# Five RMS norms of an encoder trunk: the root reaches all partitions through DRAM instead of by products

## The chip, the cores and the metric

The kernel runs on one core of a Trainium2 chip. The metric is device time of one execution in microseconds (us), the median of several runs. PE is TensorE, DVE is VectorE, ACT is ScalarE, POOL is GpSimd, SP is SyncE, which here only issues DMAs.

## The reference

One encoder layer is applied to a prompt of 1024 tokens and a sample of 256, with 256 memory tokens each, all of width 1024 and in fp32. Every sub-layer starts with the same norm:

```python
def rmsnorm(x, w):
    xf = x.astype(jnp.float32)
    y = xf * lax.rsqrt(jnp.mean(xf * xf, -1, keepdims=True) + EPS)
    return (y * w.astype(jnp.float32)).astype(x.dtype)
...
    h = rmsnorm(x, norm_mix_w)
    proj = h @ w_in
...
    x = x + merged @ w_out
    x = x + memory_cross_attention(rmsnorm(x, norm_xa_w), rmsnorm(mem, norm_mem_w), xa_w_q, xa_w_kv, xa_w_o)
    h = rmsnorm(x, norm_ffn_w)
    gu = h @ ffn_w_gate_up
    x = x + (jax.nn.silu(gu[..., :D_FF]) * gu[..., D_FF:]) @ ffn_w_down
```

The merged value comes from a gated DeltaNet branch (with beta and decay inputs per token and head) and a spatial gating branch (gMLP). A last `rmsnorm` follows the layer and gives the output.

## The kernel before

**Layout.** Activations lie transposed: the 1024 features are 8 tiles (index k) of 128 partitions, tokens lie along the free axis. Tokens form three blocks: blocks 0 and 1 are 512 prompt tokens each, block 2 is the sample's 256. A norm over features is therefore a sum over partitions and over the 8 tiles.

**Products.** Every fp32 operand is split into a high part (rounded on ACT, line 125) and a low part (the difference, on DVE or POOL, line 126), and each product is three matmuls (line 108, which all PE work shows as its line). The names hi, lo, whi and wlo are such halves. A 128x512 slice of weights or activations that DVE or POOL splits late holds up PE at its matmuls.

**Order.** PE's order is the order in which the program emits it. A clock in the program (`K.clock`, in units of about a nanosecond of PE time) decides when a side job may emit its next piece: a job is a generator, and `yield 2800` means that it goes on when PE has been given 2800 more. The orders of DVE, ACT, POOL and SP are made by the framework's scheduler, and each engine then executes its own order strictly. A DMA that SP issues and that has to wait holds up what stands behind it on SP.

**The norm.** `Norm.add` sums squares into the tile nacc. `Norm.rest` (lines 262 to 295) then waits `lag`, sums over partitions by products with a column of ones (line 275) into a PSUM bank, and computes the root on DVE in four columns (lines 231 to 235: 1 + 9 small steps) into the tile nst, 128x4: token 128c+p lies in partition p, column c. After `lag2` it brings the root to all partitions along the free axis: four products of a broadcast column with the identity (lines 279 to 281) into a bank pb of 128x512. Then come the rows, one for each k: normally a DVE operation x * weight * pb (line 294). In the two final norms some of the rows are "shared": ACT multiplies by the weight (line 289) and POOL by the root (line 290). POOL needs the root in SBUF, so ACT copies pb into nacc first (line 286). Each row goes to a sink: a split into hi and lo, a write to DRAM (memory norm), or the output.

**The five norms.** The memory norm runs early, beside the projections of the two gates and the gMLP branch (tiles gt, ug, vg) and the computation of beta and decay (tile wk, lines 543 to 562, whose last result gm PE uses as an operand). The feed-forward norms of blocks 0 and 1 run behind the attention's output projection, whose results DVE adds to x at line 1483; x2 is then stored to DRAM by SP (line 1513). The final norms of blocks 1 and 0 run in the last 90 us, behind the second feed-forward product; there DVE adds that product's banks to x at line 2246 and splits weights and activations (tiles wlo, gs) that PE uses soon after. Their shared rows are 1, 3, 5, 7 for block 1 and 1, 4, 6 for block 0. Three norms keep their products in both kernels: the first norms of blocks 0 and 1, and the feed-forward norm of block 2.

Of the kernel before, what the change touches and what calls it, by code (L numbers as in the profile page):

```python
# [167 lines left out]
def trunk_kernel(ctx: ExitStack, tc: tile.TileContext, a):  # L168
# [68 lines left out]
    class Norm:  # L237
# [21 lines left out]
                (eng or V).tensor_tensor(out=self.acc, in0=self.acc, in1=sq, op=ALU.add)  # L259
            self.k += 1  # L260

        def rest(self, xk, wcol, sink, pace=1300, shared=(), lag=1500, ks=range(KT), inplace=False, ready=None, halves=1, lag2=2800, rooms=()):

            p, n = self.p, self.n
            nb = n // P
            yield lag
            pc = bank()
            parts = [self.acc[:, i * n : (i + 1) * n] for i in range(halves)]
            if self.apart is not None:
                parts.append(self.apart)  # L270
            for c in range(nb):
                for t in parts:
                    mm(pc[:, c : c + 1], t[:, c * P : (c + 1) * P], one, t is parts[0], t is parts[-1])
            y = p.tile([P, 4 if p is xp else 16], F32, tag="nst", name="nst", bufs=2)[:, :nb]
            ms, sc = pc[:, 4 : 4 + nb], pc[:, 8 : 8 + nb]
            V.tensor_scalar(out=ms, in0=pc[:, :nb], scalar1=1.0 / D, scalar2=EPS, op0=ALU.mult, op1=ALU.add)
            rsqrt(y, ms, sc)
            yield lag2
            pb = bank()
            for c in range(nb):  # L280
                mm(pb[:, c * P : (c + 1) * P], y[:, c : c + 1].to_broadcast([P, P]), ident)
            while ready is not None and not ready():
                yield 300
            if shared:
                rb = self.acc
                S.activation(rb, pb[:, :n], AF.Copy)
            for k in ks:
                if k in shared:
                    S.activation(xk(k), xk(k), AF.Copy, scale=sm[:, wcol + k : wcol + k + 1])
                    G.tensor_tensor(out=xk(k), in0=xk(k), in1=rb, op=ALU.mult)  # L290
                    sink(k, xk(k))
                    continue
                t = bank() if k in rooms else xk(k) if shared or inplace else p.tile([P, 512], F32, tag="nsq", name="nt", bufs=self.sq)[:, :n]
                V.scalar_tensor_tensor(out=t, in0=xk(k), scalar=sm[:, wcol + k : wcol + k + 1], in1=pb[:, :n], op0=ALU.mult, op1=ALU.mult)  # L294
                sink(k, t)
                yield pace * n / 512
# [12 lines left out]
        rsqrt(y, ms, sc)  # L309
        yield lag2  # L310

    def norm(p, xk, n, wcol, sink, pace=1300, step=700, lag=1500):
        nm = Norm(p, n)
        for k in range(KT):
            nm.add(xk(k))
            yield step
        yield from nm.rest(xk, wcol, sink, pace, lag=lag)

    def to_h(h, b, mine=(1, 3, 5, 7)):
        return lambda k, t: split(h[b][0][:, k, :], h[b][1][:, k, :], t, V if k in mine else G)  # L320
# [139 lines left out]
    def other_norms():  # L460
# [7 lines left out]
        done.add(1)  # L468
        mem = x_load(a["memT"], 0, 512, "mem")
        yield 6000  # L470
        yield from norm(xp, lambda k: mem[:, k, :], 512, S_MEM, lambda k, t: SY.dma_start(md[k], t))

    norms = K.side(other_norms())

# [975 lines left out]
    class OutProj:  # L1450
# [21 lines left out]
        def run(self, xsrc, scale, wcol, xpool, store, sinks=None, then=None, after=None):  # L1472
# [24 lines left out]
            for b, (t0, n) in enumerate(BLOCKS):  # L1497
# [17 lines left out]
                if sinks is None:  # L1515
                    norm_b = nms[b].rest(xk, wcol, to_h(hs, b), 600)
                else:
                    norm_b = nms[b].rest(xk, wcol, sinks(b, hs), PACES[b], ks=range(KT) if b != 1 else SECOND_KS, inplace=True, lag2=LAGS2[b])
                K.pending[id(hs), b] = K.side(norm_b)
            self.x = x  # L1520

# [759 lines left out]
    def last_norm(nm, b):  # L2281
# [3 lines left out]
            (SY if k % 2 else S).dma_start(a["yT"][:, k, t0 : t0 + n], t)  # L2285

        if b < 2:
            K.side(nm.rest(lambda k: x2[b][:, k, :], S_FIN, sink, PACEF, SHARED[b], LAGF[b], lag2=LAGF2[b]))
            return
        pb = bank()  # L2290
        ms, y = pb[:, :n], pb[:, n : 2 * n]
# [118 lines left out]
MIX = 6500  # L2410
A1, A2, A3, A4 = 1200, 800, 2000, 600
DEC, CONV = 1200, 600
FIRST_W, PACES, LAGS2 = 9000, (600, 1300, 600), (2800, 9500, 9500)
LAGX = (26000, 17000, 9000)
FIRST_V = (1, 3, 5, 6, 7)
LAG0, LAGF, LAGF2, PACEF = 9700, (8000, 6000, 1500), (9000, 9000, 2800), 1000
# [81 lines left out]
```

## Time and profile before

| what | value |
|---|---|
| median of 3 runs | 2188.0 us (2187.18 to 2189.63) |
| profiled execution | 2189.87 us |
| its span | 2188.1 us |
| granted PE clock, mean | 0.998 |
| root done, memory norm | 95.07 us |
| root products of the five norms, start | 95.25, 1300.24, 1341.87, 2099.51, 2133.48 us |

The span runs from the first to the last recorded instruction; the profiled execution took 1.8 us more than it. Times in the tables of the trace are us from the start of the span. In the fences below, a row of the timeline is: start, duration, engine, line, operation, output<-inputs, and how many instructions were put together; in square brackets how long the engine had been idle and what released it.

### The profile page before, as it was taken

The numbers are of one execution on the slowest core, as the hardware profiler recorded it, in microseconds if no ns is written. First come the engines' busy times: TensorE is split into PE (matmuls) and PEld (weight loads), VectorE is DVE, ScalarE is ACT, GpSimd is POOL, SyncE is SP. The second block draws the span as 40 slices with busy tenths as digits, with TensorE's granted clock in tenths as the row PEclk, the third lists the DMA queues.
The fourth block names the chain that finished last, engine by engine and source line by source line (L and its number), as shares of the span: only waits on it lengthen the run. The fifth ranks groups of instructions, "written<-read, shape, count | busy, mean of one in ns | idle before, by whom it ended". The sixth has DMA issues, their size and how long they took to land.

```text
span 2188.1 us, 31978 instructions
## 1 busy us (share of the span) xinstructions
PE 2170.4 (99%) x12184; PEld 1888.5 (86%) x12184; DVE 1357.0 (62%) x2615; ACT 885.8 (40%) x1651; POOL 592.7 (27%) x399
## 2 busy tenths in 40 slices
PE   9999999999999999999999999999999999999998
PEld 8988888888988888888988888888888888888888
DVE  7867688786874845687644546644434444378575
ACT  6533363544535553124544533332322323343454
POOL 2010100101001010042412432566666665200031
PEclk9999999999999999999999999999999999999999
DMA  5221423323244546741522421222222222493531
GB/s 194 92 93 58 112 64 91 83 65 95 73 124 119 175 127 203 246 148 41 191 68 102 168 96 64 104 83 87 82 77 80 83 98 90 143 347 122 206 112 58
DMA packets 196600, 255.14 MB, mean 117 GB/s; under 512 B 77188, under 2 KB 111572, under 8 KB 196446
## 3 DMA queue, kind: packets, MB, share of 16 engines
q1 hardware_dynamic: 179038, 228.19, 32.0%
q10 hardware_dynamic: 17408, 24.91, 3.1%
q8 instruction: 95, 1.56, 0.3%
q14 instruction: 59, 0.48, 0.1%
HBM read 179.07 MB, written 73.99 MB: 116 GB/s over the span
## 4 chain that ended last, share of the span: by engine, by line
PE 92%; DVE 4%; DMA 3%; ACT 1%; issue 1%; SPq 0%; POOL 0%; DVEq 0%; ACTq 0%; POOLq 0%
PE bank L108 91%; PE bank L121 1%; DMA t<-sgd 1%; DMA braw<-gq 1%; DMA raw<-in_w_sv 0%; DVE gb L820 0%; DMA tbd<-stage 0%; DVE U L949 0%; DVE nt L294 0%; ACT junk L518 0%; DVE aT L815 0%; DMA gb<-grd 0%; DVE lo L126 0%; DMA stage<-gtd 0%; DVE bank L294 0%
## 5 line engine op out<-in xcount | busy, mean ns | idle before, releaser
L108 PE MATMUL bank<-hi,whi 128*128 128x512 f32 (+1 forms) x1976 | 700.4, 354 | 0.2 <-DVE vg L494 0.2
L108 PE MATMUL bank<-lo,whi 128*128 128x512 f32 (+1 forms) x1976 | 686.9, 348 | 0.0
L108 PE MATMUL bank<-hi,wlo 128*128 128x512 f32 (+1 forms) x1976 | 686.6, 347 | 0.0
L108 PEld LDWEIGHTS bank<-hi,wlo 128*128 128x128 f32 x1976 | 373.6, 189 | 48.0
L108 PEld LDWEIGHTS bank<-hi,whi 128*128 128x128 f32 x1976 | 374.4, 189 | 45.8 <-issue 1.4
L108 PEld LDWEIGHTS bank<-lo,whi 128*128 128x128 f32 x1976 | 374.5, 190 | 43.0
L126 POOL TENSOR_TENSOR wlo<-raw,whi 128x1024 fp32r<-128x1024 f32 x65 | 158.0, 2432 | 293.3 <-ACT whi L125 289.2
L125 ACT ACTIVATE whi<-raw 128x1024 fp32r<-128x1024 f32 (+1 forms) x136 | 137.0, 1009 | 241.6 <-PE bank L108 216.3
L126 DVE TENSOR_TENSOR wlo<-raw,whi 128x1024 fp32r<-128x1024 f32 (+1 forms) x71 | 82.5, 1164 | 73.2 <-ACT whi L125 65.9
L108 PE MATMUL bank<-bhl,whi 128*128 128x512 f32 x408 | 126.0, 390 | 0.1
L126 POOL TENSOR_TENSOR wlo<-x,whi 128x1024 fp32r<-128x1024 f32 x40 | 96.6, 2414 | 47.5 <-ACT whi L125 47.5
L2128 DVE TENSOR_TENSOR x<-x,bank 128x512 f32<-128x512 f32 x21 | 14.5, 689 | 124.7 <-ACT x L1923 124.7
L108 PEld LDWEIGHTS bank<-bhl,whi 128*128 128x128 f32 x408 | 76.4, 188 | 16.5 <-ACT whi L125 0.5
L698 DVE SCALAR_TENSOR_TENSOR acc<-craw,sm,acc 128x510 f32<-128x510 f32 (+1 forms) x96 | 73.4, 765 | 24.6 <-ACT acc L696 22.8
L1936 DVE SCALAR_TENSOR_TENSOR t<-t,x 128x512 f32<-128x512 f32 x42 | 63.9, 1520 | 28.7 <-ACT t L1935 28.7
L108 PE MATMUL bank<-bhl,wlo 128*128 128x512 f32 x204 | 79.7, 391 | 0.8 <-DVE wlo L126 0.8
L125 ACT ACTIVATE whi<-x 128x1024 fp32r<-128x1024 f32 (+1 forms) x48 | 49.2, 1024 | 77.5 <-PE bank L108 69.6
L1945 DVE SCALAR_TENSOR_TENSOR t<-bank,t 128x512 f32<-128x512 f32 (+1 forms) x44 | 24.5, 558 | 81.4 <-PE bank L108 81.4
L108 PE MATMUL bank<-bhl,ahl 128*128 128x512 f32 x312 | 75.0, 395 | 0.0
L1070 ACT ACTIVATE gs<-bank 128x512 f32<-128x512 f32 (+1 forms) x60 | 31.2, 519 | 101.2 <-PE bank L108 94.3
L1923 ACT ACTIVATE x<-bank 128x512 f32<-128x512 f32 x63 | 37.6, 597 | 82.4 <-PE bank L108 79.8
L108 PEld LDWEIGHTS bank<-bhl,ahl 128*128 128x128 f32 x312 | 58.7, 188 | 13.7
(420 smaller groups left out, 4466.9 us busy)
## 6 DMA issues: line engine op xcount, KB each, us to landing
raw<-in_w_gu SPq DMA_DIRECT2D x44, 512.0 KB, 3.4
braw<-gq SPq DMA_DIRECT2D x14, 1024.0 KB, 8.2
raw<-in_w_g SPq DMA_DIRECT2D x20, 512.0 KB, 3.3
gq<-t SPq DMA_DIRECT2D x33, 256.0 KB, 2.1
gtd<-gs ACTq DMA_DIRECT2D x32, 256.0 KB, 2.2
w<-in_w_dn SPq DMA_DIRECT2D x8, 1024.0 KB, 9.7
raw<-in_w_qkv SPq DMA_DIRECT2D x12, 512.0 KB, 3.6
gq<-r SPq DMA_DIRECT2D x22, 256.0 KB, 2.0
```

Of the source, the lines that this page charges most:

```text
L108: self.nc.tensor.matmul(out, l, r, start=start, stop=stop, skip_group_check=more)
L121: self.nc.tensor.transpose(out, x, ident)
L125: self.last_hi = self.nc.scalar.activation(hi, src, AF.Copy).ins
L126: (eng or self.nc.vector).tensor_tensor(out=lo, in0=src, in1=f32(hi), op=ALU.subtract)
L698: V.scalar_tensor_tensor(out=dst, in0=src, scalar=wj, in1=dst, op0=ALU.mult, op1=ALU.add)
L1070: S.activation(t, ps, AF.Tanh, scale=0.5)
L1923: S.activation(t, ps, AF.Copy)
L1936: V.scalar_tensor_tensor(out=t, in0=t, scalar=1.0, in1=src, op0=ALU.add, op1=ALU.mult)
L1945: V.scalar_tensor_tensor(out=out, in0=u, scalar=sign, in1=t, op0=ALU.mult, op1=ALU.mult)
L2128: V.tensor_tensor(out=c22, in0=c22, in1=pe, op=ALU.add)
```

## The change

Five norms get a row of a DRAM tile, rows_d (5x512). For them `Norm.rest` does not emit the four products. Right after the root, SP writes the 128x4 tile nst into the row (512 values of four bytes, in token order) and reads the row back into all 128 partitions of nacc (128x512, 256 KB). Then the job waits `lag2`, and the rows take nacc where they took the bank pb. ACT's copy into nacc is left out. The memory norm's `lag2` goes from 2800 to 9000, that of feed-forward block 0 from 2800 to 6500; the other three are 9500, 9000 and 9000 in both kernels.

```diff
-        def rest(self, xk, wcol, sink, pace=1300, shared=(), lag=1500, ks=range(KT), inplace=False, ready=None, halves=1, lag2=2800, rooms=()):
+        def rest(self, xk, wcol, sink, pace=1300, shared=(), lag=1500, ks=range(KT), inplace=False, ready=None, halves=1, lag2=2800, rooms=(), row=None):
...
             rsqrt(y, ms, sc)
-            yield lag2
-            pb = bank()
-            for c in range(nb):
-                mm(pb[:, c * P : (c + 1) * P], y[:, c : c + 1].to_broadcast([P, P]), ident)
+            if row is not None:
+                pb = self.acc
+                SY.dma_start(row[:n].rearrange("(c p) -> p c", p=P), y)
+                SY.dma_start(pb, row[:n].unsqueeze(0).to_broadcast([P, n]))
+                yield lag2
+            else:
+                yield lag2
+                pb = bank()
+                for c in range(nb):
+                    mm(pb[:, c * P : (c + 1) * P], y[:, c : c + 1].to_broadcast([P, P]), ident)
             while ready is not None and not ready():
                 yield 300
             if shared:
                 rb = self.acc
-                S.activation(rb, pb[:, :n], AF.Copy)
+                if row is None:
+                    S.activation(rb, pb[:, :n], AF.Copy)
...
+    rows_d = dp.tile([5, 512], F32, name="rows_d")
...
-        yield from norm(xp, lambda k: mem[:, k, :], 512, S_MEM, lambda k, t: SY.dma_start(md[k], t))
+        yield from norm(xp, lambda k: mem[:, k, :], 512, S_MEM, lambda k, t: SY.dma_start(md[k], t), lag2=9000, row=rows_d[0])
...
-                    norm_b = nms[b].rest(xk, wcol, sinks(b, hs), PACES[b], ks=range(KT) if b != 1 else SECOND_KS, inplace=True, lag2=LAGS2[b])
+                    norm_b = nms[b].rest(xk, wcol, sinks(b, hs), PACES[b], ks=range(KT) if b != 1 else SECOND_KS, inplace=True, lag2=LAGS2[b], row=rows_d[1 + b] if b < 2 else None)
...
-            K.side(nm.rest(lambda k: x2[b][:, k, :], S_FIN, sink, PACEF, SHARED[b], LAGF[b], lag2=LAGF2[b]))
+            K.side(nm.rest(lambda k: x2[b][:, k, :], S_FIN, sink, PACEF, SHARED[b], LAGF[b], lag2=LAGF2[b], row=rows_d[3 + b]))
...
-FIRST_W, PACES, LAGS2 = 9000, (600, 1300, 600), (2800, 9500, 9500)
+FIRST_W, PACES, LAGS2 = 9000, (600, 1300, 600), (6500, 9500, 9500)
```

The lines of the kernel after the change are 7 to 9 higher: the rows are on line 301 instead of 294, POOL's on 297 instead of 290, gm on 571 instead of 562, the vg operation on 532 instead of 523, the splits stay on 126.

PE's order is the same but for the five groups. The scheduler moves operations of the other engines only near the five norms. On DVE, behind the start of the beta and decay chain of the first stage, this stood before (wk and sums are small tiles of that chain and of the gMLP norm):

```order
L515 TENSOR_SCALAR sums<-sums 128x4
L545 SCALAR_TENSOR_TENSOR wk_1281<-wk_1281 128x80
L557 TENSOR_SCALAR wk_1281<-wk_1281 128x80
L549 TENSOR_SCALAR wk_1281<-wk_1281 128x80
L550 RECIPROCAL wk_1281<-wk_1281 128x80
L551 TENSOR_TENSOR wk_1281<-wk_1281 128x80
L552 TENSOR_TENSOR wk_1281<-wk_1281 128x80
L553 TENSOR_SCALAR wk_1281<-wk_1281 128x80
```

The same stretch of DVE's order now (nt is a row of the memory norm):

```order
L524 TENSOR_SCALAR sums<-sums 128x4
L301 SCALAR_TENSOR_TENSOR nt<-mem,sm,nacc 128x512
L566 TENSOR_SCALAR wk_1267<-wk_1267 128x80
L558 TENSOR_SCALAR wk_1267<-wk_1267 128x80
L559 RECIPROCAL wk_1267<-wk_1267 128x80
L301 SCALAR_TENSOR_TENSOR nt<-mem,sm,nacc 128x512
L560 TENSOR_TENSOR wk_1267<-wk_1267 128x80
L561 TENSOR_TENSOR wk_1267<-wk_1267 128x80
L562 TENSOR_SCALAR wk_1267<-wk_1267 128x80
```

The last two of the eight memory rows are seen here inside the chain; two more stand a few rows earlier, where before all eight stood ahead of the chain. At the end of that chain DVE had, before:

```order
L235 SCALAR_TENSOR_TENSOR sums<-sums 128x4
L556 SCALAR_TENSOR_TENSOR wk_1281<-wk_1281 128x80
L233 SCALAR_TENSOR_TENSOR sums<-sums 128x4
L558 SCALAR_TENSOR_TENSOR wk_1281<-wk_1281 128x80
L234 TENSOR_TENSOR sums<-sums 128x4
L492 SCALAR_TENSOR_TENSOR gt<-gt,bank 128x512
L562 SCALAR_TENSOR_TENSOR gm<-wk_1281,rows 128x8x4
```

And now, up to the same gm:

```order
L235 SCALAR_TENSOR_TENSOR sums<-sums 128x4
L503 SCALAR_TENSOR_TENSOR ug<-gt,bank 128x512
L564 SCALAR_TENSOR_TENSOR wk_1267<-wk_1267 128x80
L233 SCALAR_TENSOR_TENSOR sums<-sums 128x4
L565 SCALAR_TENSOR_TENSOR wk_1267<-wk_1267 128x80
L234 TENSOR_TENSOR sums<-sums 128x4
L567 SCALAR_TENSOR_TENSOR wk_1267<-wk_1267 128x80
L235 SCALAR_TENSOR_TENSOR sums<-sums 128x4
L571 SCALAR_TENSOR_TENSOR gm<-wk_1267,rows 128x8x4
```

The 128x512 operation on gt (line 492, now 501) went up in the order, and the one that makes ug (now 503) stands ahead of gm. In the final norm of block 0 DVE had, behind the root (hi, lo and w are loaded weights of which the splits make wlo):

```order
L126 TENSOR_TENSOR wlo<-w_17296,whi 128x512 x4
L126 TENSOR_TENSOR wlo<-hi_17294,whi 128x512
L294 SCALAR_TENSOR_TENSOR x_17299<-x_17299,sm,bank 128x512
L126 TENSOR_TENSOR wlo<-hi_17294,whi 128x512
L294 SCALAR_TENSOR_TENSOR x_17299<-x_17299,sm,bank 128x512 x2
L126 TENSOR_TENSOR wlo<-hi_17294,whi 128x512
L294 SCALAR_TENSOR_TENSOR x_17299<-x_17299,sm,bank 128x512 x2
L126 TENSOR_TENSOR wlo<-hi_17294,whi 128x512
```

The same stretch now:

```order
L126 TENSOR_TENSOR wlo<-w_17288,whi 128x512 x4
L301 SCALAR_TENSOR_TENSOR x_17291<-x_17291,sm,nacc 128x512 x2
L126 TENSOR_TENSOR wlo<-hi_17286,whi 128x512
L301 SCALAR_TENSOR_TENSOR x_17291<-x_17291,sm,nacc 128x512 x2
L126 TENSOR_TENSOR wlo<-hi_17286,whi 128x512
L301 SCALAR_TENSOR_TENSOR x_17291<-x_17291,sm,nacc 128x512
L126 TENSOR_TENSOR wlo<-hi_17286,whi 128x512 x2
```

Two rows now stand ahead of the first of the four hi splits, two ahead of the second and one ahead of the third.

More of the change, by code (lines that the diff above doesn't have):

```diff
@@ L310, in rstd_of, with norm @@
         yield lag2
-    def norm(p, xk, n, wcol, sink, pace=1300, step=700, lag=1500):
+    rows_d = dp.tile([5, 512], F32, name="rows_d")
+    def norm(p, xk, n, wcol, sink, pace=1300, step=700, lag=1500, **kw):
         nm = Norm(p, n)
@@ L316, in norm @@
             yield step
-        yield from nm.rest(xk, wcol, sink, pace, lag=lag)
+        yield from nm.rest(xk, wcol, sink, pace, lag=lag, **kw)
     def to_h(h, b, mine=(1, 3, 5, 7)):
```

## The prediction

> **What bounds the kernel now.** I read the page first, for the engine that is never idle; then the groups of the tile that holds the root, for what is removed; then the PE timeline at one of the five places, for what that costs in PE time.
>
> ```profile
> span 2188.1 us, 31978 instructions
> PE 2170.4 (99%) x12184; PEld 1888.5 (86%) x12184; DVE 1357.0 (62%) x2615; ACT 885.8 (40%) x1651; POOL 592.7 (27%) x399
> ```
> ```profile
> L108 PE MATMUL bank<-cst,nst x60: 270/275/376, 30.6 to 2134.3; 128*128 128x128 f32 x60
> ```
> ```profile
> 95.25 1.05 PE L108 MATMUL bank<-cst,nst 128*128 128x128 f32 x8
> 96.06 0.37 PE L108 MATMUL bank<-svh,hi 128*128 128x264 f32 x1
> 96.26 0.28 PE L108 MATMUL bank<-svh,lo 128*128 128x264 f32 x1
> 96.38 0.29 PE L108 MATMUL bank<-svl,hi 128*128 128x264 f32 x1
> ```
>
> PE is busy for 99% of the span, so a microsecond counts only if PE loses or gains it. Matmuls are pipelined: what one costs is the distance to the next start. The group of the memory norm (4 fp32 products, 8 records) takes from 95.25 to 96.06, 0.81 us, and the product behind it takes 0.20 us to the next start where its neighbour takes 0.12. One group is worth 0.81 + 0.08 = 0.89 us.
>
> **What is removed.** Five such groups go: 5 x 0.89 = 4.45 us, 0.2% of the time. That is the whole gain on offer, because nothing else leaves PE: its order is otherwise the same. ACT's copies at L286 go too, but PE does not wait for them once the rows come by DMA. About 0.2% (4.4 us) is also what a measurement of this kernel can tell from no change. So the question is which of the five places gives its 0.89 back, and more.
>
> **What is added: a round trip.** SP writes the 128x4 root as 512 pieces and reads it back as 128 rows of 2 KB. Neither is in the trace; the nearest transfers are these (KB each, us from issue to landing).
>
> ```profile
> gb<-grd SPq DMA_DIRECT2D x10, 512.0 KB, 4.0
> stage<-gtd SPq DMA_DIRECT2D x16, 256.0 KB, 3.1
> xsd<-gb SPq DMA_DIRECT2D x40, 32.0 KB, 1.7
> ```
>
> The write is small, like xsd (1.7 us); the read moves 256 KB, like stage (3.1). I take 1.7 + 3.1 = 4.8 us; bounds 3.4 (twice 1.7) and 1.7 + 4.0 = 5.7. Whether that is hidden depends on the lag between root and rows; I go through the places below.
>
> **What is added: a lock.** The rows (L294 before, L301 after) now take both operands from SBUF, where the second came from PSUM. Two groups of DVE operations (ns minimum/median/maximum) show what that means:
>
> ```profile
> L294 DVE SCALAR_TENSOR_TENSOR x<-x,sm,bank x33: 467/737/748, 1302.8 to 2140.7; 128x512 f32<-128x512 f32 x25, 128x256 f32<-128x256 f32 x8
> L1945 DVE SCALAR_TENSOR_TENSOR x<-x,t x21: 685/1666/1667, 1402.7 to 1904.9; 128x512 f32<-128x512 f32 x21
> ```
>
> With PSUM the longest of 33 is 748 ns, beside POOL or not; with two SBUF operands the median is 1666, because DVE stands until POOL's operation is through. The Trainium skill ("SBUF — State Buffer", section "Who interferes with whom") says that such an operation and a GpSimd operation that reads SBUF exclude each other for a whole instruction. The rows agree (748 against 1666), and by a chip without this rule the terms for the two final norms below would be zero. It speaks against this change.
>
> **Memory norm (lag 2800 to 9000).** Columns: start, us, operation, idle time before it.
>
> ```profile
> 94.91 0.16 DVE L235 SCALAR_TENSOR_TENSOR nst<-bank,nst 128x4 f32<-128x4 f32 x1
> 96.41 1.41 DVE L294 SCALAR_TENSOR_TENSOR nt<-mem,sm,bank 128x512 f32<-128x512 f32 x2 [1.25 <-issue]
> ```
> ```profile
> 109.55 2.35 DVE L234 TENSOR_TENSOR sums<-sums 128x4 f32<-128x4 f32 x1
> ...
> 112.09 0.24 DVE L556 SCALAR_TENSOR_TENSOR wk<-wk 128x80 f32<-128x80 f32 x1
> ...
> 112.37 0.24 DVE L558 SCALAR_TENSOR_TENSOR wk<-wk 128x80 f32<-128x80 f32 x1
> ...
> 112.60 0.68 DVE L492 SCALAR_TENSOR_TENSOR gt<-gt,bank 128x512 f32<-128x512 f32 x1
> 113.20 0.45 DVE L562 SCALAR_TENSOR_TENSOR gm<-wk,rows 128x32 f32<-128x32 f32 x4
> ...
> 114.81 3.98 DVE L523 TENSOR_SCALAR vg<-vg,sums 128x512 f32<-128x512 f32 x4
> ```
> ```profile
> 109.46 2.43 POOL L126 TENSOR_TENSOR wlo<-raw,whi 128x1024 fp32r<-128x1024 f32 x1 [35.38 <-ACT whi L125]
> 115.02 2.57 POOL L126 TENSOR_TENSOR wlo<-raw,whi 128x1024 fp32r<-128x1024 f32 x1 [3.13 <-ACT whi L125]
> ```
> ```profile
> 115.45 0.63 PE L108 MATMUL bank<-cst,gm 128*40 128x128 f32 x4
> ...
> 117.89 1.45 PE L108 MATMUL bank<-sw,vg 128*128 128x128 f32 x8
> 119.09 0.48 PE L108 MATMUL bank<-hi,whi 128*128 128x512 f32 x1
> ```
>
> The root is done at 95.07, so the row lands near 99.9 and the first memory row starts 3.5 us later than now (96.41). Nobody needs those rows soon. But DVE works in order, and now four of the eight rows (1.41 / 2 = 0.7 us each) stand among the small steps of the beta and decay chain that ends in gm, which PE uses at 115.45. That chain already lost 2.35 us to POOL's first subtraction (109.46 to 111.89). After, PE is 0.89 earlier and ACT hands POOL its input a little earlier; I let POOL hold the lock from 108.9 to 111.3. Delayed by 4 x 0.7 = 2.8 us, the chain is then caught further up, at the step behind the reciprocal, with some 12 dependent steps left, where before it had three or four. A step is 112.37 - 112.09 = 0.28 us. About six of them, and the gt row of 0.6, end at 113.6. From the end of the gt row (113.28 before) POOL's second subtraction starts 115.02 - 113.28 = 1.74 us later, so at 115.35. From the same point gm still needs five or six steps and the ug row, 2.1 us. It misses POOL's start by 0.4 us and stands until 115.35 + 2.57 = 117.9; gm ends near 118.4 instead of 113.65.
>
> PE wants gm at 115.45 - 0.89 = 114.56 and starts 3 us later than in before. It gets 0.4 back at the sw,vg group, whose 8 records took 1.45 us there against 1.05 for the 8 of the root, a wait for vg. So PE is 2.6 us behind the old time, a wait of 3.5. If gm slips in ahead of POOL, vg is next: it starts after gm, about 2 us later than 114.81, and ends 2 us later, a wait of 2.0 + 0.89 = 2.9. Least is a wait of 2.0, if POOL comes early, most 4.0, if PE gets nothing back. I take **3.2 us**.
>
> A pause of that length can also cost clock. Columns of the windows: PE, PEld, DVE, ACT and POOL busy, granted clock, DMA share, GB/s.
>
> ```profile
> 879.00:882.00 3.00, 0.90 (x6) 0.48 (x5) 2.36 (x4) 0.67 (x2) 0.00 (x0) 1.00 1.04 401
> 882.00:884.00 2.00, 2.00 (x12) 2.00 (x11) 1.66 (x4) 0.12 (x1) 0.00 (x0) 0.56 0.80 232
> 884.00:886.00 2.00, 2.00 (x7) 1.56 (x6) 0.96 (x2) 0.94 (x1) 0.00 (x0) 0.59 0.90 322
> ```
>
> There PE stood for about 2 of 3 us, and 4 us at 0.56 and 0.59 followed: 2 x 0.44 + 2 x 0.41 = 1.7 us lost. The next such pause may or may not draw it; between 0 and 1.7 I take **0.8 us**. The Trainium skill ("TensorE: Matmul & The Clock Gate", "Part 1: The HAM clock gate (the "warmup" mystery)") names an idle window of about 3.4 us as what lowers the clock. By it the sum would be without the 0.8; the trace disagrees, a shorter pause was enough.
>
> **Feed-forward norms of blocks 0 and 1.**
>
> ```profile
> 1302.76 2.72 DVE L294 SCALAR_TENSOR_TENSOR x<-x,sm,bank 128x512 f32<-128x512 f32 x4 [0.87 <-DMA x2d<-x]
> ...
> 1317.01 0.69 DVE L1483 SCALAR_TENSOR_TENSOR x<-bank,x 128x512 f32<-128x512 f32 x1 [2.92 <-PE bank L108]
> ...
> 1357.15 0.69 DVE L126 TENSOR_TENSOR wlo<-x,whi 128x512 fp32r<-128x512 f32 x1
> ```
> ```profile
> 1363.68 0.39 PE L108 MATMUL bank<-whi 128*128 128x512 f32 x1
> ```
>
> Block 0's read stands on SP behind the store of x2 for which the old rows waited until 1302.76; I put its landing 3.7 us later, at 1306.5. The eight rows are late by that, and locked against POOL's splits, which costs at most as much again as the two or three POOL operations among them. On DVE the evacuations L1483 stand behind them; before, DVE had idled 2.92 us by the one at 1317.01, and PE has four banks of 5.4 us each ahead of it, so this is absorbed. PE reads these rows only in the feed-forward stage, and block 1's lag of 9500 is twice the round trip, so its rows keep their time and only the lock is new. The last split of the stage ended at 1357.84 and PE used it at 1363.68: 5.8 us in hand, less 0.89. Both norms: **0**, bounds 0 and 1 us, if an evacuation is late after all.
>
> **Final norm, block 1.** Half its rows go through POOL (L290).
>
> ```profile
> 2101.30 2.72 DVE L294 SCALAR_TENSOR_TENSOR x<-x,sm,bank 128x512 f32<-128x512 f32 x4 [2.70 <-ACT nacc L286]
> ...
> 2113.00 0.69 DVE L2246 SCALAR_TENSOR_TENSOR x<-bank,x 128x512 f32<-128x512 f32 x1 [0.67 <-PE bank L108]
> ```
> ```profile
> 2101.34 5.51 POOL L290 TENSOR_TENSOR x<-x,nacc 128x512 f32<-128x512 f32 x4 [14.66 <-ACT nacc L286]
> ```
> ```profile
> 2113.87 0.40 PE L108 MATMUL bank<-gs,whi 128*128 128x256 f32 x2
> ```
>
> Row landing: I take 2100.2 (the same 4.8 behind this norm's root, and one pair of reads stands between write and read on SP). The first row starts 1.1 us earlier than now, but DVE's four and POOL's four alternate. A POOL operation takes 5.51 / 4 = 1.4 us beside DVE, 1.2 alone, a row 0.65: 1.85 us a pair, four pairs to 2107.6. Behind them DVE has six splits and four evacuations, ten times 0.6 us: the last ends at 2113.6. PE needs it at 2113.87 - 0.89 = 2112.98. Loss **0.6 us**, bounds 0 (POOL late, DVE's rows first) and 2.
>
> **Final norm, block 0.**
>
> ```profile
> 2126.95 0.16 DVE L235 SCALAR_TENSOR_TENSOR nst<-bank,nst 128x4 f32<-128x4 f32 x1
> ...
> 2133.14 0.69 DVE L126 TENSOR_TENSOR wlo<-hi,whi 128x512 fp32r<-128x512 f32 x1 [0.75 <-ACT whi L125]
> ```
> ```profile
> 2135.30 4.26 POOL L290 TENSOR_TENSOR x<-x,nacc 128x512 f32<-128x512 f32 x3 [17.79 <-ACT nacc L286]
> ```
> ```profile
> 2137.84 0.28 PE L108 MATMUL bank<-gs,wlo 128*128 128x256 f32 x1
> ```
>
> The root ends at 2127.11, the row lands at 2131.9. Two rows now stand on DVE ahead of the first wlo<-hi split, with POOL's three between them: three pairs of about 1.9 us, so the split ends at 2137.7 instead of 2133.83. PE wants it at 2137.84 - 0.89 = 2136.95: 0.8 late, and the next split about 0.5 more. Loss **1.3 us**, 0 to 2.2.
>
> **Sum.** -4.45 + 3.2 + 0.8 + 0 + 0.6 + 1.3 = +1.45 us. The profiled run took 2189.87 (span 2188.1), so it would come to 2191.3; from the median of 2188.0, 1.9 below it, 2189.4.
>
> **Rivals.** (a) *Room enough.* DVE idles 38% of the span (1357 us busy), and if rows give way everywhere PE gets all five groups: 2188.0 - 4.45 = 2183.5. For it: feed-forward lags are long. Against it: gm's steps follow one upon another, idle share is no help there. Chance 0.12. (b) *Only the memory stage pays*, at 2.0 without a clock loss, or only the final norms pay: -4.45 + 2.0 = -2.5 or -4.45 + 1.9 = -2.6, 2185.5. Chance 0.22. (c) *Slower: the row comes too late for the final norm of block 0.* DVE stands in order at its first row, with the splits PE lives on behind it. It decides once the read lands past 2133.4, a round trip over 6.3 us, a little past my 5.7 (DMA is heavily used there). Each us more is a us of PE; landing at 2135 costs 3 more, and with the pause at its 4.0 and 1.7 the sum is -4.45 + 4.0 + 1.7 + 0.6 + 1.3 + 3 = +6.2: 2194.2. Chance 0.14. My forecast keeps 0.52.
>
> **The range.** Low 2183.4, the full gain; high 2192.5, my sum with the upper end of the memory terms (0.8 + 0.9) and of the last norm (0.9) is 2192.0, and half a us for the feed-forward bound. It leaves out (c) and little else. Faster by over 0.2%: most of (a), 0.11. Slower: (c) and a little of my own, 0.15. Within: 0.74.
>
> **What would show it.** In the profile after: no bank<-cst,nst at the five places; row landings 4 to 6 us behind the roots; L301 with medians over 1 us at the final norms; gm behind POOL's second subtraction; PE idle 2 to 4 us near 114.5, perhaps a low clock after it. I am wrong if gm comes before 115.4, or PE keeps its 0.12 us steps from 2112 to 2140.

## The result, and the profile after

The changed kernel took 2240.59 us (median of 5 runs, 2238.59 to 2242.6) against 2188.44 before: a ratio of 1.024, interval 1.0229 to 1.0251. That is 52 us more, where 2189.4 had been forecast and 2192.5 was the upper end. The profiled execution has a span of 2238.1 us, 50.0 more than before.

The page, busy time and the shares of the chain that ended last (engines, then lines):

```profile
PE 2178.4 (97%) x12144; PEld 1894.6 (85%) x12144; DVE 1361.8 (61%) x2615; ACT 884.5 (40%) x1649; POOL 596.4 (27%) x399
PE 84%; DVE 7%; DMA 6%; ACT 1%; issue 1%; SPq 0%; POOL 0%; DVEq 0%; ACTq 0%; POOLq 0%
```

The 40 records of the five groups are gone (12184 to 12144), and PE is idle for 3% instead of 1%. DMA and DVE now have 13% of the chain, where they had 7%. So something new waits on a DMA. SP's timeline at the memory norm shows which: line 280 is the write of the root, line 281 the read that needs it.

```profile
95.32 0.37 SPq L280 DMA_DIRECT2D rows_d<-nst  x1
105.47 0.32 SPq L281 DMA_DIRECT2D nacc<-rows_d  x1
```

SP could issue the read only 10.15 us after the write. The read itself behaves as expected (DMA view, KB each, us to landing):

```profile
nacc<-rows_d SPq DMA_DIRECT2D x5, 256.0 KB, 3.3
```

DVE stands in order at its first row of each of the five norms (idle time and releaser in brackets):

```profile
109.79 0.75 DVE L301 SCALAR_TENSOR_TENSOR nt<-mem,sm,nacc 128x512 f32<-128x512 f32 x1 [9.61 <-DMA nacc<-rows_d]
...
1327.92 1.41 DVE L301 SCALAR_TENSOR_TENSOR x<-x,sm,nacc 128x512 f32<-128x512 f32 x2 [7.78 <-DMA nacc<-rows_d]
...
1369.39 0.75 DVE L301 SCALAR_TENSOR_TENSOR x<-x,sm,nacc 128x512 f32<-128x512 f32 x1 [8.26 <-DMA nacc<-rows_d]
...
2138.50 5.79 DVE L301 SCALAR_TENSOR_TENSOR x<-x,sm,nacc 128x512 f32<-128x512 f32 x4 [11.23 <-DMA nacc<-rows_d]
...
2180.83 3.52 DVE L301 SCALAR_TENSOR_TENSOR x<-x,sm,nacc 128x512 f32<-128x512 f32 x2 [8.68 <-DMA nacc<-rows_d]
```

From the write's issue to the first row that is 14.5 us at the memory norm (95.32 to 109.79), 14.2 at feed-forward block 1 and 14.6 at the final norm of block 1. The prediction had 4.8. DVE idles 45.6 us in all. PE waits for what is queued behind those rows:

```profile
118.70 0.58 PE L108 MATMUL bank<-hi,whi 128*128 128x256 f32 x1 [5.66 <-ACT whi L125]
...
121.46 0.58 PE L108 MATMUL bank<-hi,wlo 128*128 128x256 f32 x1 [1.96 <-POOL wlo L126]
...
128.05 1.07 PE L108 MATMUL bank<-cst,gm 128*40 128x128 f32 x4 [3.46 <-DVE gm L571]
...
1347.62 0.59 PE L108 MATMUL bank<-cst,nacc 128*128 128x1 f32 x2 [4.30 <-DVE nacc L259]
...
1376.42 0.80 PE L108 MATMUL bank<-cst,nacc 128*128 128x1 f32 x3 [7.24 <-DVE nacc L259]
...
2149.27 0.76 PE L108 MATMUL bank<-gs,whi 128*128 128x256 f32 x2 [8.50 <-DVE x L2255]
...
2186.07 0.58 PE L108 MATMUL bank<-gs,wlo 128*128 128x256 f32 x1 [9.21 <-DVE wlo L126]
```

The first two are for splits of weights that ACT began late. ACT had itself stood, in order, for a DVE operation behind the row:

```profile
112.63 0.41 ACT L502 ACTIVATE gt<-gt 128x248 f32<-128x248 f32 x1 [10.00 <-DVE gt L501]
```

PE's seven waits sum to 40.3 us. Each is followed by some microseconds at a lower clock. The windows (granted clock is the third number from the end) behind four of them:

```profile
119.00:126.00 7.00, 3.64 (x15) 3.05 (x14) 6.86 (x22) 3.60 (x8) 3.16 (x2) 0.61 0.34 113
...
1350.00:1357.00 7.00, 7.00 (x48) 7.00 (x48) 5.12 (x13) 2.73 (x4) 3.37 (x2) 0.76 0.41 145
1376.00:1384.00 8.00, 7.58 (x27) 6.30 (x28) 6.63 (x18) 3.01 (x5) 0.00 (x0) 0.71 0.37 131
2150.00:2156.00 6.00, 5.47 (x28) 5.22 (x27) 5.38 (x7) 5.14 (x10) 5.59 (x4) 0.55 0.57 188
```

Since PE's order is the same but for the five groups, the start of each PE instruction after can be set against its start before. This displacement is worked out from the two traces, and its steps say where the time went:

| place (time in before) | step, us |
|---|---|
| memory norm (group gone at 95; stage at 110 to 120) | -0.90, +14.33 |
| pause near 880, which also differs between runs of like code | +1.11 |
| feed-forward norms, 1300 to 1360 | -0.93, +6.76, +6.82, +1.77 |
| final norm, block 1, 2100 to 2120 | -0.88, +11.94 |
| final norm, block 0, 2130 to 2140 (net) | +10.12 |
| all, with small steps | +49.8 |

The first numbers confirm 0.89 us a group. 50.0 + 4.45 us saved makes 54.5 us of new loss: 40.3 of waits in the rows above, and the other 14 mostly the lower clock behind them: PE's busy time grew by 8.0 us although 4.45 us of its work are gone.

### The profile page after: what moved, and what is told of

It reads as the page before. It is cut to its first block, busy times and chain, and to the rows that moved or that the text cites. A ratio compares the mean times of both kernels' runs of the same rounds, so it can differ in the third digit from the quotient of the medians.

```text
span 2238.1 us, 31908 instructions
## 1 busy us (share of the span) xinstructions
PE 2178.4 (97%) x12144; PEld 1894.6 (85%) x12144; DVE 1361.8 (61%) x2615; ACT 884.5 (40%) x1649; POOL 596.4 (27%) x399
## 4 chain that ended last, share of the span: by engine, by line
PE 84%; DVE 7%; DMA 6%; ACT 1%; issue 1%; SPq 0%; POOL 0%; DVEq 0%; ACTq 0%; POOLq 0%
PE bank L108 82%; DMA rows_d<-nst 2%; PE bank L121 1%; DMA nacc<-rows_d 1%; DVE x L301 1%; DMA t<-sgd 1%; DMA braw<-gq 1%; DVE W L856 0%; DMA tbd<-stage 0%; DVE nacc L259 0%; DVE W L859 0%; DVE wlo L126 0%; DVE lo L126 0%; DVE nt L301 0%; DMA stage<-gtd 0%
## 5 line engine op out<-in xcount | busy, mean ns | idle before, releaser
L126 POOL TENSOR_TENSOR wlo<-x,whi 128x1024 fp32r<-128x1024 f32 x40 | 96.6, 2414 | 47.2 <-ACT whi L125 47.2
L2137 DVE TENSOR_TENSOR x<-x,bank 128x512 f32<-128x512 f32 x21 | 14.5, 688 | 125.2 <-ACT x L1932 125.2
L108 PE MATMUL bank<-gs,whi 128*128 128x256 f32 x352 | 67.3, 294 | 9.0 <-DVE x L2255 9.0
```

The costliest lines, as they stand in the source:

```text
L108: self.nc.tensor.matmul(out, l, r, start=start, stop=stop, skip_group_check=more)
L126: (eng or self.nc.vector).tensor_tensor(out=lo, in0=src, in1=f32(hi), op=ALU.subtract)
L2137: V.tensor_tensor(out=c22, in0=c22, in1=pe, op=ALU.add)
```

## The experiments

Three theories. W: the write of 4-byte pieces completes late, so the round trip is three times as long as assumed, and DVE stands in order. L: the rows that read SBUF twice wait for POOL. Q: SP or its queue is held up by what else stands there. Ratios are against the kernel before on the same chip.

**e1, the write by itself.** Products kept; at each of the five norms this stands behind the root:

```diff
+                each = lines.rearrange("(c p) w -> p c w", p=P)[:, :, :1]
+                for store, view in ((tiny.rearrange("(c p) -> p c", p=P), y), (wide.rearrange("(p c) -> p c", c=4), y), (each, y.unsqueeze(2)), (narrow.unsqueeze(1), y[:, :1])):
+                    SY.dma_start(store, view)
+                    SY.dma_start(view, store)
```

> The kernel before (products kept) with four writes from SBUF to DRAM at each of the five norms, each followed on SP by a read that needs it: 512 pieces of 4 bytes side by side (tiny, as in the change), 128 pieces of 16 bytes side by side (wide), 512 pieces of 4 bytes 64 bytes apart (lines), 128 pieces of 4 bytes side by side (narrow). What counts is the time from the write's issue to the issue of its read; the kernel's own time says nothing. Theory W (the write of small pieces is slow to complete): tiny 9 to 11 us at all five places; if pieces that share 64 bytes of DRAM wait for each other, lines 2 to 3 us and wide and narrow in between (4 pieces share 64 bytes: 3 to 5 us; 32 pieces: near tiny); if it is the number of pieces, lines like tiny and wide and narrow near 3 us. Rival Q (SP or its queue is held up by what stands there, not by this write): all four alike at a place, and different from place to place.

SP's timeline at the memory norm; from the start of a write to that of the read behind it:

```profile
96.32 0.37 SPq L282 DMA_DIRECT2D tiny<-nst  x1
105.46 0.37 SPq L283 DMA_DIRECT2D nst<-tiny  x1
107.92 0.33 SPq L282 DMA_DIRECT2D wide<-nst  x1
109.34 0.33 SPq L283 DMA_DIRECT2D nst<-wide  x1
111.66 0.37 SPq L282 DMA_DIRECT2D lines<-nst  x1
113.45 0.37 SPq L283 DMA_DIRECT2D nst<-lines  x1
115.44 0.33 SPq L282 DMA_DIRECT2D narrow<-nst  x1
122.36 0.33 SPq L283 DMA_DIRECT2D nst<-narrow  x1
```

9.14 us for the 512 pieces side by side, 1.42 for 16-byte pieces (less than the 3 to 5 expected), 1.79 for the same 512 pieces 64 bytes apart, 6.92 for a quarter of the pieces side by side. At the other four places: 8.2 to 9.2, 1.4, 1.8 to 2.2, 7.1 to 7.4. Q falls, since places do not matter. Neither the number of pieces nor their size alone does it (512 pieces of 4 bytes take 1.8 us when apart); it is small pieces close together.

**e9, how close.** The same with other distances.

```diff
+                for step, store in zip((2, 4, 8, 16), probe):
+                    each = store.rearrange("(c p) w -> p c w", p=P)[:, :, :1]
+                    SY.dma_start(each, y.unsqueeze(2))
+                    SY.dma_start(y.unsqueeze(2), each)
+                pairs = probe[4].rearrange("(h p c) -> p h c", p=P, c=2)
...
```

> As in the first probe, a write and a read that needs it, one behind the other on SP, at each of the five norms; the kernel's own time says nothing. 512 pieces of 4 bytes at distances of 8, 16, 32 and 64 bytes (8, 4, 2 and 1 pieces in 64 bytes of DRAM; side by side it was 16), then 256 pieces of 8 bytes side by side (8 in 64 bytes). If pieces in the same 64 bytes wait for each other: about 9.1 / 16 = 0.57 us each, so 4.6, 2.3 to 2.8, 2 and 1.8 us, and 4.6 for the pieces of 8 bytes. Rival (only pieces that touch each other are slow): about 1.8 at all four distances, and 9 or so for the pieces of 8 bytes.

The first two pairs of the timeline at the memory norm (8 and 16 bytes apart), then all places:

```profile
95.08 0.37 SPq L281 DMA_DIRECT2D by<-nst  x1
99.48 0.37 SPq L282 DMA_DIRECT2D nst<-by  x1
101.34 0.36 SPq L281 DMA_DIRECT2D by<-nst  x1
104.25 0.36 SPq L282 DMA_DIRECT2D nst<-by  x1
```

| pieces of 4 bytes in 64 bytes | write to read, us, five places |
|---|---|
| 16 (e1) | 8.2 to 9.2 |
| 8 | 3.2 to 4.4 |
| 4 | 2.6 to 2.9 |
| 2 | 1.8 to 2.2 |
| 1 | 1.8 to 2.2 |
| 8-byte pieces, 8 in 64 bytes | 3.0 to 4.1 |

The time grows with the number of pieces that share 64 bytes, not in proportion, but much as expected; the rival (only touching pieces) falls at 8 and 4. By what unit they collide (64 bytes or more) was not tried, and the count in 64 bytes is not all: in e1 pieces of 16 bytes, four in 64 bytes, took 1.42 us, here four pieces of 4 bytes take 2.6 to 2.9 (128 pieces there, 512 here). The Trainium skill ("DMA: Bandwidth & Descriptors", section "Specifications") states that transfers under 512 bytes are done as read-modify-write. That would fit a queue of writes to one spot. But pieces of 16 bytes took 1.4 us here, so being under 512 bytes is not what decides.

**e5, the change with pieces of 16 bytes.** Column c of the root holds tokens 4p+c, so a partition's four values lie together in DRAM. The orders on DVE and SP are the change's.

```diff
-                    mm(pc[:, c : c + 1], t[:, c * P : (c + 1) * P], one, t is parts[0], t is parts[-1])
+                    mm(pc[:, c : c + 1], t[:, c : n : nb] if row is not None else t[:, c * P : (c + 1) * P], one, t is parts[0], t is parts[-1])
...
-                SY.dma_start(row[:n].rearrange("(c p) -> p c", p=P), y)
+                SY.dma_start(row[:n].rearrange("(p c) -> p c", c=nb), y)
```

> The change with one thing different: column c of the root holds tokens 4p+c instead of 128c+p, so that SP writes 128 pieces of 16 bytes instead of 512 of 4. The orders of DVE, ACT, POOL and SP are those of the change. The probe had 1.4 us for such a write against 9.1. Theory W: the round trip falls to about 1.4 + 3.3 = 4.7 us, what the prediction assumed (4.8), and the time comes to the prediction's sum with the lock at its measured size (8.3 instead of 1.9 for the rows from SBUF): 2188 to 2197 us, 43 to 52 us under the change. Rival L (lock and the rows' places in DVE's order, which are all kept here): above 2215 us.

2202.19 us, ratio 1.0068 (1.0056 to 1.0081): 14.9 us over the kernel before instead of 52. L, which would have kept most of the loss, falls as the main cause: at least 37 of 52 us are the write. But 14.9 is more than expected (at most 9.5). The timeline of the memory stage shows DVE hardly waiting for the row, and then the prediction's own story; DVE first, then PE, then the window behind (clock third from the end):

```profile
101.39 0.75 DVE L301 SCALAR_TENSOR_TENSOR nt<-mem,sm,nacc 128x512 f32<-128x512 f32 x1 [0.65 <-DMA nacc<-rows_d]
...
109.92 2.44 DVE L560 TENSOR_TENSOR wk<-wk 128x80 f32<-128x80 f32 x1
...
116.21 2.34 DVE L567 SCALAR_TENSOR_TENSOR wk<-wk 128x80 f32<-128x80 f32 x1
```
```profile
118.91 1.07 PE L108 MATMUL bank<-cst,gm 128*40 128x128 f32 x4 [3.51 <-DVE gm L571]
```
```profile
119.00:125.00 6.00, 6.00 (x25) 5.29 (x26) 4.71 (x13) 1.29 (x3) 0.00 (x0) 0.50 0.28 94
```

Only at the final norm of block 1 does DVE still stand for the row for longer, 3.95 us: the row starts 7.3 us behind the write's issue there (2103.59 to 2110.92) and 5.5 at the memory norm, against the 4.8 of the prediction. In the memory stage POOL catches the chain at L560 and at L567, gm comes 3.5 us late, and the clock is 0.50 for 6 us behind it. The displacement of PE at the five places:

| place | predicted, us | e5, us | of it strided sums |
|---|---|---|---|
| memory norm | -0.89 + 3.2 + 0.8 = +3.1 | +0.98 - 0.90 + 5.97 = +6.1 | 0.98 |
| feed-forward norms | -1.8 | +0.84 - 0.93 + 2.45 - 0.88 + 1.36 = +2.8 | 0.84 + 2.45 |
| final norm, block 1 | -0.89 + 0.6 = -0.3 | +0.86 - 0.92 + 2.93 = +2.9 | 0.86 |
| final norm, block 0 | -0.89 + 1.3 = +0.4 | +0.95 - 0.88 + 1.43 = +1.5 | 0.95 |

The last column is this edit's own doing: the sums now load weights in steps of 16 bytes. Groups of the tile nacc (ns minimum/median/maximum), before and e5:

```profile
L108 PEld LDWEIGHTS bank<-cst,nacc x76: 186/192/192, 55.0 to 2122.8; 128*128 128x128 f32 x76
```
```profile
L108 PEld LDWEIGHTS bank<-cst,nacc x76: 186/308/332, 54.8 to 2134.3; 128*128 128x128 f32 x76
```

332 instead of 192 ns, eight times a norm, and about 0.9 us in the displacement at each, 4.6 in all. Behind one of them, the sums of feed-forward block 1, the clock also dropped without any wait of PE:

```profile
1335.00:1340.00 5.00, 5.00 (x27) 5.00 (x28) 3.36 (x10) 1.36 (x2) 1.97 (x1) 0.68 0.83 324
```

That is another 1.6 us (0.32 of 5). e10 to e12, which have strided sums too, show the same step of 2.5; e13 and e14 below, without them, show none. But e6 has the same strided sums there and a step of 0.97 at full clock, so that the sums alone do not lower it, and the cause of the low clock stays open. So 4.6 us of the 14.9 are the edit's, or 6.1 with this clock, and 10.3 or 8.8 the change's with a short round trip.

**e2, a longer lag.** Pieces of 4 bytes.

```diff
-    ... lag2=9000, row=rows_d[0])
+    ... lag2=16000, row=rows_d[0])
-... LAGS2 = ... (6500, 9500, 9500)
+... LAGS2 = ... (16000, 16000, 9500)
-... LAGF2, PACEF = ... (9000, 9000, 2800), 1000
+... LAGF2, PACEF = ... (16000, 16000, 2800), 1000
```

> The change with the lag between root and rows at 16000 for all five norms, longer than the measured round trip of 12 to 15 us. Theory W: DVE no longer stands at the rows, most of the 52 us goes: 2184 to 2200 us. Rival L (rows that read SBUF twice and wait for POOL are what costs): the rows are as many and read the same, the time stays above 2215 us. Rival Q: SP still stands before each read, but nothing on DVE waits, like W.

2235.2 us, ratio 1.0218 (1.0202 to 1.0233). W as I had put it is wrong on this: lags longer than the round trip help by 5 us. The time is also where L had put it, above 2215 us, but e5 has ruled L out as the main cause. DVE's timeline, first row of the final norm of block 1:

```profile
2132.36 5.83 DVE L301 SCALAR_TENSOR_TENSOR x<-x,sm,nacc 128x512 f32<-128x512 f32 x4 [10.08 <-DMA nacc<-rows_d]
```

Still 10.1 us of standing. The lag decides when the program emits the rows; DVE's order is the scheduler's, and in four of the five norms the rows did not move in it (they moved in feed-forward block 0). A lag in the program hides nothing that the scheduler's order does not.

**e4, e7, e8, the change at one place each** (pieces of 4 bytes; the others keep products and lags). The norms that stay as they were get no `row`, as here the final ones:

```diff
-... row=rows_d[3 + b]))
+...))
```

> The change at the memory norm alone (lag 9000, through DRAM); the other four keep products and lags. Theory W: the waits of PE in this stage (6.0 + 2.4 + 3.9 us), the low clock behind them (about 5) and 0.9 saved: 2188.4 + 16, so 2200 to 2208 us. Rival L with the round trip of the prediction: 2190 to 2193 us.

> The change (pieces of 4 bytes) at the two feed-forward norms alone. Theory W: PE's two waits there (4.6 and 7.6 us) and the low clock behind them (about 3), less 1.8: 2199 to 2204 us. The prediction had these two places at 2186.2.

> The change (pieces of 4 bytes) at the two final norms alone. Theory W: the rest of the 52 us, 8.9 and 9.5 us of waits and a low clock behind them, less 1.8: 2208 to 2216 us, so that the three parts (12.8 for the memory norm) add up to about 52. Rival L with a short round trip: 2190 to 2194.

| kernel | median, us | ratio (interval) | loss, us |
|---|---|---|---|
| memory norm alone | 2200.73 | 1.0062 (1.0045 to 1.0078) | 13.6 |
| feed-forward norms alone | 2199.38 | 1.0058 (1.0045 to 1.0071) | 12.7 |
| final norms alone | 2207.92 | 1.0095 (1.0081 to 1.0108) | 20.8 |

The loss is ratio less 1 times the kernel before. The three sum to 47.1, and the change lost 52.5 by its ratio: the parts are nearly independent, and each is where the displacement puts it (13.4, 14.4 and 21.2). The final norms came just under what was expected.

**e3, the lock by itself.** The kernel before; ACT copies the bank to SBUF and all rows of the five norms read the copy.

```diff
+            if copy or shared:
                 rb = self.acc
                 S.activation(rb, pb[:, :n], AF.Copy)
+                if copy:
+                    pb = rb
```

> The kernel before with its products and lags; in the five norms ACT copies the bank to SBUF and all rows read that copy, so the rows are locked against POOL as in the change, and nothing goes through DRAM. Theory W: the lock alone costs what the prediction put on the final norms, about 2 us, and little at the memory norm, whose rows stay ahead of the chain: 2188 to 2194 us. Rival L: above 2210 us.

2196.18 us, ratio 1.0035 (1.0022 to 1.0048): 7.7 us by the ratio. More than the 0 to 6 expected of W and far from L's 22. In the displacement 5.0 of it are at the final norms (+3.71 and +1.25) and 3.3 in the memory stage, where PE's timeline has

```profile
119.15 1.86 PE L108 MATMUL bank<-sw,vg 128*128 128x128 f32 x8 [1.22 <-DVE vg L525]
```
```profile
2117.02 0.50 PE L108 MATMUL bank<-gs,whi 128*128 128x256 f32 x2 [1.60 <-DVE x L2248]
```

DVE's rows of the final norm of block 1 show the lock itself: these four took 2.72 us in the kernel before, behind the same wait for ACT's copy.

```profile
2102.94 6.98 DVE L296 SCALAR_TENSOR_TENSOR x<-x,sm,nacc 128x512 f32<-128x512 f32 x4 [2.71 <-ACT nacc L286]
```

So the lock is real, and with the low clock behind PE's wait (0.70 and 0.50 from 2117 to 2121) it costs more than the prediction had for the final norms: 5.0 us, not 1.9. At these two norms ACT's copy for POOL was there before as well, so this is the lock alone. At the memory norm the copy is new, and is not told apart from the lock.

**e6, only the feed-forward norms, pieces of 16 bytes** (edits of e5 and e7 together).

> Pieces of 16 bytes, and only the two feed-forward norms go through DRAM (block 0 with its lag of 6500); the memory norm and the final norms keep their products. Theory W with the prediction's reading of these two places (all hidden): 2 x 0.89 us saved, 2185.5 to 2188 us. Rival: the lock shows here as well: 2189 to 2192 us.

2189.77 us, ratio 1.0012 (1.0003 to 1.0021). The rival: about 2.6 us over the kernel before, where 1.8 should have been saved. In its displacement the two groups give 1.8 us, the strided sums take 0.84 + 0.97 (the clock granted is 1.00 from 1325 to 1345) and the stretch with block 1's rows 1.7, so the rival has half of the loss and the edit itself the other half.

**e10, rows ahead of the chain; e11, rows from PSUM; e12, both** (all on e5).

```diff
-        yield 6000
+        yield 1000
         yield from norm(xp, lambda k: mem[:, k, :], ...
```
```diff
+            if row is not None:
+                pb = bank()
+                S.activation(pb[:, :n], self.acc, AF.Copy)
```

> Pieces of 16 bytes, and the memory norm starts about 5 us earlier (its first yield is 1000 instead of 6000), so that all eight of its rows stand ahead of the beta and decay chain in DVE's order, as in the kernel before. If the rows' place inside the chain is what PE waited for at gm with pieces of 16 bytes (3.8 us, and 3 us of low clock behind it), that wait goes: 2202.2 - 6 to 7, 2194 to 2198 us. Rival (POOL catches the chain whatever stands ahead of it): the wait stays, 2200 to 2204 us.

> Pieces of 16 bytes; ACT copies the row from SBUF to a PSUM bank, and the rows on DVE read the bank as in the kernel before, so that they do not wait for POOL; the rows' places stay. If the lock on the rows is what is left at the final norms (about 3.5 us of the 14.9), that goes, and the memory stage stays: 2196 to 2200 us. Rival (what is left is the later landing and the order): 2201 to 2204 us.

> Pieces of 16 bytes, the memory norm earlier and the rows from PSUM: both edits together. If both causes are right and nothing else is left, the products' 4.45 us show as a gain or nearly so: 2184 to 2190 us. Rival: above 2193 us, then the later landing itself still costs.

e10: 2200.18, ratio 1.0058 (1.0044 to 1.0072); e11: 2201.97, 1.0068 (1.0055 to 1.0081); e12: 2198.72, 1.0054 (1.0042 to 1.0067). All three missed. In e10 the wait at gm is gone, as its windows there show, PE busy 7.00 of 7 and 6.00 of 6 at full clock:

```profile
112.00:119.00 7.00, 7.00 (x39) 6.04 (x37) 6.86 (x27) 3.50 (x6) 2.78 (x2) 1.00 0.22 77
119.00:125.00 6.00, 6.00 (x36) 4.72 (x35) 5.35 (x7) 1.15 (x3) 2.21 (x1) 1.00 0.31 94
```

But the earlier norm made PE wait for its sum of squares instead, with a low clock behind:

```profile
86.81 2.03 PE L108 MATMUL bank<-cst,nacc 128*128 128x1 f32 x8 [1.94 <-DVE nacc L259]
```
```profile
88.00:92.00 4.00, 4.00 (x21) 4.00 (x22) 1.54 (x7) 0.39 (x1) 0.00 (x0) 0.67 0.17 66
```

The step at 80 to 90 is +5.6, of which 0.9 is only the sums' products, which the edit moves up; the stage as a whole comes to +3.8, where e5 has +6.1. PE thus reaches gm 3.6 us later than before, but the chain is also short again: from its first operation on wk to the end of gm DVE takes 8.8 us (108.49 to 117.26), as before (104.87 to 113.64), where e5 took 12.9 (106.10 to 119.04). So the rows' place in the chain is what made it long, and the edit is no cure. In e11 the final norm of block 1 lost 2.1 instead of 2.9 and that of block 0 0.5 instead of 1.4, but the memory stage 0.7 more (ACT's copy comes first), and the pause near 880 took 1.0 where e5 had happened to gain 2.0. The lock on DVE's rows is worth under 2 us at the final norms here, and a median does not show it. What is left in e12, 11.8 us by its ratio and 11.0 in the displacement, is the memory stage (+4.9, most of it the wait that the earlier norm makes), the feed-forward norms (+1.8) and the final norms (+4.6), strided sums and saved groups counted in. At the final norm of block 1 e12 has a step of 3.7 where e11 has 2.1 with the same rows: behind PE's wait the clock is 0.52 for 3 us in e12 and stays at 1.00 in e11.

**e13, pieces of 16 bytes without strided sums.** The root is written as it lies, and the rows read the 128x512 row with the tokens turned back.

```diff
-                SY.dma_start(row[:n].rearrange("(c p) -> p c", p=P), y)
+                SY.dma_start(row[:n].rearrange("(p c) -> p c", c=nb), y)
...
+                turn = lambda t: t.rearrange("q (c p) -> q c p", p=P)
+                rb = pb = self.acc.rearrange("q (p c) -> q c p", c=nb)
```

> Pieces of 16 bytes again, but the sums keep their contiguous weights: the root is written as it lies, 16 bytes a partition, and the rows (DVE and POOL) read the 128x512 row with the token order turned back in their access pattern. The orders of all engines are those of the change. In the first such kernel the sums by strided weights took 0.9 us more at each norm in the profile. Theory: those 4.4 us go, 2202.2 - 4.4 = 2197.8, 2195 to 2200 us; the rest, some 10 us over the kernel before, is rows in the chain with the low clock behind it, lock and later rows. Rival (the strided sums lay beside other waits, or turned rows are slower on DVE): 2200 to 2204 us.

2211.66 us, ratio 1.011 (1.0096 to 1.0124): the rival, and more. Reading steps of 16 bytes made each row on DVE longer, 1145 ns where it was 743 in e5, and POOL's operations, which DVE's rows hold up, went from 1741 to 2392:

```profile
L305 DVE SCALAR_TENSOR_TENSOR x<-x,sm,nacc x25: 1118/1145/2571, 1312.1 to 2160.3; 128x512 f32<-128x512 f32 x25
```

The kernel does not isolate what it was meant to; that the strided sums cost 4.6 to 6.1 us in e5 rests on the profiles.

**e14, the detour where it should be harmless.** As e13, but the memory norm keeps its products, and ACT copies the row into a bank in token order, from which DVE's rows read.

```diff
-... lag2=9000, row=rows_d[0])
+...)
...
+                pb = turn(bank()[:, :n])
+                S.activation(pb, rb, AF.Copy)
```

> As that kernel, but the memory norm keeps its products and its lag of 2800, and in the other four ACT copies the row into a PSUM bank, from which DVE's rows read. So 4 x 0.89 = 3.6 us of products go, no row stands in the chain, no row on DVE waits for POOL. Theory (each part of the 14.9 us has been named): within 0.2% of the kernel before, 2185 to 2190 us. Rival (something else in the detour through DRAM costs): above 2192 us.

2186.9 us, ratio 0.9997 (0.9988 to 1.0006). The expectation holds: four groups are gone, DVE's rows are as short as before, and the time is the same within what can be told:

```profile
L307 DVE SCALAR_TENSOR_TENSOR x<-x,sm,bank x33: 467/739/749, 1305.7 to 2137.4; 128x512 f32<-128x512 f32 x25, 128x256 f32<-128x256 f32 x8
```

In the displacement the four groups give 3.6 us and 2.7 are lost again, 1.3 at the feed-forward norms and 1.4 at the final norm of block 1. No version beat the kernel before beyond doubt.

## Why the prediction was wrong

**The gain was right.** 0.89 us a group; the displacement has 0.88 to 0.93 at each place. 4.45 us was all that these groups could give.

**The step that failed is the round trip.** The prediction put the write at 1.7 us, from the row xsd<-gb, "The write is small, like xsd (1.7 us)", with 3.4 and 5.7 as bounds of the whole. Measured: 10.15 for the write, about 4 for the read, 13.9 to 14.6 in all. That row was no such write: each of its transfers is 256 pieces of 128 bytes, as the kernel (line 831) and its packets show, where the root is 512 pieces of 4 bytes, 16 of them in 64 bytes. e1 and e9 show that small pieces lying so close are what counts. No row of the trace showed such a write, so the upper bound had no ground and the range was too narrow. With pieces of 16 bytes (e5) 37 of 52 us go, although that edit adds some of its own.

**The rival that had the mechanism** was (c): DVE in order at its first row, what PE lives on queued behind. It was priced at one norm, with 3 us, and needed a round trip of 6.3. It happened at all five, at over twice that.

**"block 1's lag of 9500 is twice the round trip, so its rows keep their time"** failed twice: in the size, and because the lag does not set DVE's order (e2).

**The feed-forward norms were not free.** The prediction looked at the evacuations and at the last split; PE waited for the squares of the next blocks' norms (nacc, line 259), which stand behind the rows on DVE: 4.3 and 7.2 us after the change. Of the -1.8 forecast e5 without the strided sums (and the low clock behind them) leaves -0.4, and e6 without them -0.1.

**The memory stage was right in mechanism.** With a round trip near the assumed one (e5) the chain was caught at the step behind the reciprocal and again before gm, and PE waited 3.5 us (3.2 taken). The clock behind it was mis-sized: 0.50 for 6 us, 3 us lost, against 0.8 taken and 1.7 at most. In the change itself two further waits (5.66 and 1.96) came on top, behind the late chain of DVE, ACT and POOL.

**The lock was right, its start was not.** At the final norm of block 1 the 0.6 counted on rows that start 1.1 us earlier than before. In e3 they start as before, and PE waits 1.6 us; the low clock behind that wait, for which the prediction had no term there, brings the step to 3.7. At block 0 it was 1.25, with 1.3 taken. In e5 the first row of block 1 starts 7.4 us behind the root, where it was 6.1 before, and the steps are 2.9 and 1.4; with DVE's rows out of the lock (e11) 2.1 and 0.5 are left.

With the strided sums taken off, the rows of e5's table come to 5.1 - 0.4 + 2.0 + 0.5 = +7.2 us (8.7 if the low clock at the feed-forward norms is not theirs), where the prediction's sum had +1.45. So with a round trip near the one that it assumed the prediction would still have been 6 to 7 us low, and the time above its range.

**Left open:** how many bytes of DRAM must lie between two pieces for them not to collide, what lowered the clock behind the strided sums in e5 and not in e6, and how the lock and ACT's copy share the 3.3 us of e3's memory stage.

## What to carry to other kernels

When a DMA's price is taken from another row, compare the size of a piece and how close the pieces lie, not bytes or count alone, and if no row has that shape leave the upper bound far open. A product on the busiest engine that takes 0.9 us may be cheaper than a detour, if an engine that executes in order must wait for its result: ask first what stands behind that wait. And a lag in the program is cover only if the scheduler's order moves with it.

## What the runs showed of the hardware

- 512 writes of 4 bytes to DRAM: 8.2 to 9.2 us side by side, 3.2 to 4.4 at 8 bytes apart, 2.6 to 2.9 at 16, 1.8 to 2.2 at 32 and 64 (e1, e9). In the change's trace the packets of the first such write all lie between 96.2 and 96.6, and the read could be issued at 105.47, so by these records it is the completion that comes late.
- fp32 weights loaded in steps of 16 bytes: 332 ns instead of 192 (e5). A DVE operation of 128x512 that reads one operand in such steps: 1145 ns instead of 743 (e13, e5). On POOL: 1567 (e14) instead of 1298 (before), both where DVE's rows read PSUM.
- A wait of PE of 3.5 us was followed by 6 us at half the clock (e5), one of 1.9 us, with strided sums behind it, by 4 us at 0.67 (e10), so that a wait can cost nearly twice its length. One of 1.3 us was followed by no low clock (e11), one of 1.7 us at the same place by 3 us at 0.52 (e12). Strided sums were followed by 5 us at 0.68 with no wait at all in e5, and by full clock in e6.
